# The same instructions on tiles that start at other bytes: matmul operands moved to multiples of 128

## The chip, the cores and the metric

The kernel runs on one core of one Trainium2 chip. TensorE (PE) multiplies, with its weight loads shown as an engine of their own (PEld). VectorE (DVE), ScalarE (ACT) and GpSimd (POOL) do the elementwise work. SyncE (SP) issues the transfers. The metric is the time of one execution on the device in microseconds, the median of three runs. TensorE's granted clock has two levels, 1.2 and 2.4 GHz; a share of 1.00 in the profile is the upper one.

## The reference, cut to what matters

One layer of a hybrid decoder on 512 tokens of width 1024, in float32:

```python
h = rms_norm(x, g_mix)
q, fp, iv, go, bg, cg, xc, u, v, gates = split(h @ w_in)      # 1024 x 7680
o_a = hgrn2_mix(q, fp, iv, go, lower_bounds, g_hgrn_out)      # gated linear recurrence
o_b = short_conv_mix(bg, cg, xc, w_conv)
o_c = spatial_gating_mix(u, v, sg_ln_g, sg_ln_b, w_sg, b_sg)
y = einsum('bsnw,nwd->bsnd', stack([o_a, o_b, o_c]), w_branch)
x = x + sum(sigmoid(gates) * y) @ w_o
x = x + square(relu(rms_norm(x, g_ffn) @ w_ff1)) @ w_ff2       # 1024 -> 4096 -> 1024
return rms_norm(x, g_final)
```

Nearly all of the arithmetic is in the products with `w_in`, `w_branch`, `w_o`, `w_ff1` and `w_ff2`.

## The kernel before

Activations lie with channels on the 128 partitions and the 512 tokens along the free axis, so a tile of 128 channels is 2048 bytes on each partition. Every large product is computed from split operands: a float32 value is cut into a rounded high part and the rest (`split`, L76, and `split_hi`/`split_lo`, L739 to L752; the type of both parts is float32r), and `mm3` (L88) adds three matmuls, high x high (L89), high x low (L90) and low x high (L91). One such matmul has a stationary operand of 128x128 (512 bytes on each partition, loaded by a weight load) and streams a moving operand of 128x512 through it (2048 bytes on each partition). A 1024-deep product for 128 output channels is a unit of 8 x 3 = 24 matmuls into one PSUM bank.

The work is a hand-written list of units (L537 to L555, L693 to L725). Around each unit the main loop (L858) issues the next weight tile's DMA on SP, splits the tile loaded before it on ACT and DVE, and evacuates the unit before. The recurrence, the spatial gate and the convolution hang on slots of that list (`pre`, `post`).

Where the operands lie follows from the order in which the pools hand out tiles. A tile takes a multiple of 32 bytes on each partition, and one pool's region follows the other's without a gap: first the constants (`cp`: `vec`, `cons`, `lm`, ..., `bnst`, `bnmv`), then the working pool (`wp`: three `raw`, six `tmp`, three `wh`, three `wl`, then small columns `ra` and `rr` of 16 bytes, each in a place of 32), then the slots `z`, `h` and `x` (`rp`). `raw`, `wh`, `wl` and `h` are 4096 bytes, `z` and `x` 2048. A `tmp` takes 2080 bytes, since one of its users (L489) asks for 514 columns. The constants end at byte 96 of a 128-byte line, and all that follows inherits it:

```
start modulo 128, before     raw 96 | tmp 96, 0, 32, 64, 96, 0 | wh 32 | wl 32 | z 96 | h 96 | x 96
                             ones 96 | ones_r 96 | cons 96 | wsm 96
```

Modulo 512, `wh` and `wl` start at 288, and `z`, `h` and `x` at 96. Slices of 128 or 512 columns step by multiples of 512 bytes and so keep their tile's value. The large matmuls therefore come in three kinds:

- **weights from `wh`/`wl` (32), stream from `x`, `z` or `h` (96)**: the projections, branches, output projection and the first feed-forward product; 2496 matmuls (shown as acc<-x,wh, acc<-x,wl, acc<-z,wh, acc<-z,wl, acc<-h,wh, acc<-h,wl);
- **weights from an `h` slot (96), stream from `z` (96)**: the second feed-forward product; 672 matmuls of 512 columns and 192 of 256 columns (acc<-z,h);
- **weights from `x` (96), stream from `wh`/`wl` (32)**: the two token-major products, L833 and the units of `v_mm` (L403); 192 matmuls (acc<-wh,x and acc<-wl,x).

In these names the stream stands first and the weights second. Six more float32r matmuls (L145, L146) take weights from `ones_r` (96) and stream a `tmp`; in all three at L145 that tile starts at 0. L149 is a plain float32 product of 256 columns, which the trace shows as two matmuls, each going over the columns once more slowly.

Of the kernel before, what the change touches and what calls it, by code (L numbers as in the profile page):

```python
# [7 lines left out]
F32 = mybir.dt.float32  # L8
# [5 lines left out]
P = 128  # L14
S = 512
# [21 lines left out]
def trunk_kernel(ctx: ExitStack, tc, xT, w_f, w_t, w_bc, w_a, w_o, w_1, w_2, vecs, rows, w_sg, cst, lmask, out):  # L37
    nc = tc.nc
    cp = ctx.enter_context(tc.tile_pool(name="cp", bufs=1))
    wp = ctx.enter_context(tc.tile_pool(name="wp", bufs=3))  # L40
# [7 lines left out]
    def nm(s):  # L48
        uid[0] += 1
        return f"{s}_{uid[0]}"  # L50

    def ct(shape, name, dt=F32):
        return cp.tile(shape, dt, name=name, tag=name)
# [4 lines left out]
    def zslot(i, dt):  # L58
        return rp.tile([P, S], dt, tag=f"z{i}", name=nm("z"))
# [4 lines left out]
    def acc():  # L64
        return pa.tile([P, S], F32, tag="acc", name=nm("acc"))
# [4 lines left out]
    def tt(e, o, a, b, op):  # L70
        return e.tensor_tensor(out=o, in0=a, in1=b, op=op)  # L71
# [21 lines left out]
    def cs(k, n=P):  # L93
        return slice(k * n, (k + 1) * n)

    # constants
    vec = ct([P, V_N], "vec")
    cons = ct([P, C_N], "cons")
    ident = cons[:, C_ID:C_ID + P]
# [10 lines left out]
    rb2 = ct([P, S], "rb2")  # L110

    def tmp(w=S, dt=F32):
        return wp.tile([P, w], dt, tag="tmp", name=nm("tmp"), bufs=6)

    def rsqrt_cols(src, n, inv, eps, dst):
        """dst[:, :n] = (src * inv + eps) ** -0.5"""
        a = wp.tile([P, 4], F32, tag="ra", name=nm("ra"), bufs=4)
        dve.tensor_scalar(out=a[:, :n], in0=src, scalar1=inv, scalar2=eps, op0=ALU.mult, op1=ALU.add)
        tt(pool, dst[:, :n], a[:, :n], mhalf[:, :n], ALU.pow)

    def col4():
        return wp.tile([P, 4], F32, tag="rr", name=nm("rr"), bufs=6)

    def col_sums(ps, src, n=4):
        for t in range(n):
# [2 lines left out]
    def diag(cols, n=4):  # L128
        dg = tmp()
        tt(dve, dg[:, :n * P].rearrange("p (b s) -> p b s", b=n), ident.unsqueeze(1).to_broadcast([P, n, P]),  # L130
           cols[:, :n].unsqueeze(2).to_broadcast([P, n, P]), ALU.mult)
        return dg

    def ones_hi(src):
        hi = tmp(S, F32R)
        act.activation(hi, src, AF.Copy)
        return hi

    def ones_lo(src, hi):
        lo = tmp(S, F32R)  # L140
        tt(dve, lo, src, f(hi), ALU.subtract)
        return lo
# [26 lines left out]
    units = []  # L169
# [5 lines left out]
    loads, when = [], {}  # L175
# [14 lines left out]
            return a  # L190
        return unit(w_f[j], mm, ev)

    # recurrence: decays, keys, queries
    def ev_f(h, a):
        kk[h] = zslot(2 * h, F32)
        A[h] = zslot(2 * h + 1, F32)
        hs = [hslot(h * 4 + i, F32) for i in range(4)]
        names = ("QA", "t1", "QB", "y", "q", "R", "go", "att")
        d = {n: hs[i // 2][:, cs(i % 2, S)] for i, n in enumerate(names)}
        heads.append(d)  # L200
        fp = d["QA"]
        tt(dve, fp, a, rb, ALU.mult)
        act.activation(kk[h], fp, AF.Sigmoid, scale=-1.0)
        act.activation(d["t1"], fp, AF.Abs)
        pool.memset(d["att"], 0.0)
# [55 lines left out]
            dve.tensor_scalar(out=d["y"], in0=d["y"], scalar1=al[:, h:h + 1], scalar2=cl[:, h:h + 1], op0=ALU.add, op1=ALU.max)  # L261
            tt(dve, A[h], d["y"], d["t1"], ALU.add)

    # recurrence: interactions at distance scale m = 2 ** l
    def halves(ap, m):
        v = ap.rearrange("p (b two m) -> p b two m", two=2, m=m)
        if m == 1:
            v = v[:, :, :, 0]
            return v[:, :, 0], v[:, :, 1]
        return v[:, :, 0, :], v[:, :, 1, :]  # L270
# [51 lines left out]
            mk = lm[:, cs(l)].unsqueeze(1).to_broadcast([P, 4, P])  # L322
            dve.copy_predicated(v4(d["att"]), mk, v4(d["ps"]))

    # recurrence: blocks of 128 through the state
    def far_prep(pair):
        for h in pair:
            d = heads[h]
            act.activation(d["y"][:, :3 * P], d["R"][:, :3 * P], AF.Exp)
            act.activation(d["t1"][:, P:], A[h][:, P:], AF.Exp)  # L330
        for h in pair:
            d = heads[h]
            tt(dve, d["QA"][:, :3 * P], kk[h][:, :3 * P], d["y"][:, :3 * P], ALU.mult)
            tt(dve, d["QB"][:, P:], d["q"][:, P:], d["t1"][:, P:], ALU.mult)
# [39 lines left out]
    def mix_norm(pair):  # L374
        for h in pair:
            d = heads[h]
            ss, r = col4(), col4()
            for b in range(4):
                act.activation(d["QA"][:, cs(b)], d["ps"][:, cs(b)], AF.Square, accum_out=ss[:, b:b + 1])
            rsqrt_cols(ss, 4, 1.0 / P, EPS, r)  # L380
            d["r"] = r
# [17 lines left out]
            zt[0][h] = (zslot(2 * h, F32R), zslot(2 * h + 1, F32R))  # L399
            split(d["t1"], *zt[0][h])  # L400

    # spatial gate
    def v_mm(j):  # L403
        def mm(w):
            if j == 0:
                part["v"] = [acc() for _ in range(4)]
            a4 = part["v"]
            for k2 in range(2):
                k = 2 * j + k2
                for t in range(4):  # L410
                    mm3(a4[t], xh[k][:, cs(t)], xl[k][:, cs(t)], w[0][:, cs(k2, S)], w[1][:, cs(k2, S)], k == 0, k == KD - 1)
        return mm
# [10 lines left out]

    st = ct([P, 4, 6], "bnst")
    mv = ct([P, 4, 2], "bnmv")

    def v_stats():
        for t in range(4):
            dve.bn_stats(st[:, t, :], vln[t])
            dve.bn_aggr(mv[:, t, :], st[:, t, :])  # L430

    def v_norm():
        r = col4()
        rsqrt_cols(mv[:, :, 1], 4, 1.0, LN_EPS, r)
        for t in range(4):
            dve.tensor_scalar(out=vln[t], in0=vln[t], scalar1=mv[:, t, 0:1], scalar2=r[:, t:t + 1], op0=ALU.subtract, op1=ALU.mult)
# [42 lines left out]
        zt[2][g] = (zslot(16 + 2 * g, F32R), zslot(17 + 2 * g, F32R))  # L479
        split(part["sv", g], *zt[2][g])  # L480

    # short convolution
    def ev_cg(c, a):
        y = tmp()
        part["cy"] = y
        tt(dve, y, a, rb2, ALU.mult)
# [18 lines left out]
        yield  # L505
        tt(dve, lo, y, f(hi), ALU.subtract)

    # gates, branch outputs, merge
    def ev_gate(d, n, a):
        g = tmp()  # L510
        part[n] = g
        tt(dve, g, a, rb, ALU.mult)
        act.activation(g, g, AF.Sigmoid)
# [19 lines left out]
        tt(dve, mt[:, S:], part[0], f(mt[:, :S]), ALU.subtract)  # L533
        mg.append((mt[:, :S], mt[:, S:]))

    # order of the units of tensor work
    for h in range(NH):  # L537
        proj(4 + h, lambda a, h=h: ev_f(h, a))
    for h in range(NH):
# [57 lines left out]
        at(pre, 19 + g, sg_split, g)  # L597
    at(pre, 21, go_sig)

    # output projection, residual, second norm  # L600
    x2, x2h, x2l = [], [], []

    def reload_x():
# [37 lines left out]
        ones_mm(part["c2"], part["qh"], part["ql"])  # L641

    def ffn_rows():
        """-2 * (mean square + eps) ** -0.5, on every partition"""
        a, r, t = tmp(), tmp(), tmp()
        act.activation(r, part["c2"], AF.Sqrt, scale=1.0 / D, bias=eps_c)
        dve.tensor_scalar(out=a, in0=part["c2"], scalar1=1.0 / D, scalar2=EPS, op0=ALU.mult, op1=ALU.add)
        dve.reciprocal(r, r)
        tt(pool, t, a, r, ALU.mult)
        tt(pool, t, t, r, ALU.mult)  # L650
        part["r2b"] = ct([P, S], "rb2")
        dve.scalar_tensor_tensor(out=part["r2b"], in0=t, scalar=-3.0, in1=r, op0=ALU.add, op1=ALU.mult)
# [1 line left out]
    def ffn_late():  # L654
        return [ev_1(i, held[i]) for i in range(3)]

    # feed-forward
    hid = {}

    def ev_1(i, a):  # L660
# [48 lines left out]
    at(pre, f0 + 1, ffn_split)  # L709
    at(post, f0 + 1, ffn_ss)  # L710
    at(pre, f0 + 2, ffn_rows)
    at(pre, f0 + 3, ffn_late)
    for g in range(1, NG):
# [14 lines left out]
    order = [x for s in sorted(when) for x in when[s]]  # L728
# [24 lines left out]

    held = []
    with tc.manual_schedule():
        # warm the tensor engine's clock and the activation tables while the first loads run
        dve.memset(ones, 1.0)
        pool.memset(mhalf, -0.5)
        nc.scalar.dma_start(vec, vecs)
# [2 lines left out]
        warm = acc()  # L762
        for i in range(WARM):
            pe.matmul(warm[:, :P], ones, ones, start=True, stop=True)

        # x: load, scale by the gain, split, sum of squares; the recurrence's value rows, token-major
        xr = [zslot(k, F32) for k in range(KD)]
        rw = []
        for k in range(KD):
# [17 lines left out]
        for k in range(KD + 1):  # L787
# [29 lines left out]
            if k == KD:  # L817
                cps = acc()
                col_sums(cps, sq_tot)
                rsqrt_cols(cps[:, :4], 4, 1.0 / D, EPS, rstd)  # L820
                dg = diag(rstd)
                dh = ones_hi(dg)
                dl = ones_lo(dg, dh)
# [34 lines left out]
        for i in range(len(units)):  # L858
# [27 lines left out]
            w, mm, ev = units[i]  # L886
# [4 lines left out]
                fn(*a)  # L891
        prev[0](prev[1])

        # last group of the feed-forward, by token halves, and the final norm
        g = NG - 1
        n2 = S // 2

# [31 lines left out]
        def fin_rstd():  # L929
            r = col4()  # L930
            rsqrt_cols(part["fc"][:, :2], 2, 1.0 / D, EPS, r)
            part["fd"] = diag(r, 2)
# [40 lines left out]
        warm = acc()  # L973
# [60 lines left out]
```

## Time and profile before

| | |
|---|---|
| time, median of 3 runs | 860.74 us (857.92 to 861.56) |
| profiled execution, span from first to last instruction | 859.3 us |
| its mean granted TensorE clock | 0.997 |
| PE busy | 847.2 us (99%), 3990 matmuls |
| DVE, ACT, POOL busy | 473.6, 322.3, 140.4 us |
| read from HBM | 80.83 MB, 97 GB/s over the span |

The execution's time outside of its span is not listed; the median of the runs is 1.4 us above the span. Matmuls are pipelined and their ends are modelled, so a matmul's listed duration is not what it adds to the run. What it adds is the step from its start to the next one's. The two are tied: in the timeline a matmul of 512 columns that is followed at once lasts about 163 ns more than its step, so that a mean duration of 389 ns is a step of about 226.

### The profile page before, as it was taken

To read this page: it belongs to the slowest core of one execution; us is meant where nothing else is said; L and a number is where in the kernel's file an instruction comes from. 1 tells how busy PE (TensorE), PEld (TensorE's weight loads), DVE (VectorE), ACT (ScalarE), POOL (GpSimd) and SP (SyncE) were. 2 spreads that over 40 slices of the span, in tenths; PEclk is the share of its full clock that TensorE was granted. 3 is DMA by queue.
4 is the path that set the end of the run, shared out by engine and by line. 5 is a ranking of instruction groups with operands and counts; after the bars stand their busy time and mean duration, and the time that the engine had idled before them with its cause. 6 is when DMAs were issued, how large, how long until landed. Compare 5 with 4: busy or idle time off the path is not lost.

```text
span 859.3 us, 10105 instructions
## 1 busy us (share of the span) xinstructions
PE 847.2 (99%) x3990; PEld 706.8 (82%) x3990; DVE 473.6 (55%) x623; ACT 322.3 (38%) x491; POOL 140.4 (16%) x152
## 2 busy tenths in 40 slices
PE   8999899999999999999999999999999999999997
PEld 7888788888888888888888888888888888888896
DVE  7456989978564444544445458444444444444424
ACT  6567355354333232323223446232232323232222
POOL 4313455661210000000001310000000000000034
PEclk9999999999999999999999999999999999999999
DMA  8331222212122323232235234222223232322002
GB/s 302 118 99 50 84 88 75 74 50 98 50 75 86 110 86 111 86 96 100 86 110 208 92 131 149 96 98 98 98 98 98 98 98 98 98 91 90 17 1 99
DMA packets 26256, 83.59 MB, mean 97 GB/s; under 512 B 3040, under 2 KB 3424, under 8 KB 26208
## 3 DMA queue, kind: packets, MB, share of 16 engines
q1 hardware_dynamic: 26064, 82.91, 29.1%
q8 instruction: 31, 0.51, 0.2%
q14 instruction: 17, 0.14, 0.1%
q10 hardware_dynamic: 144, 0.03, 0.0%
HBM read 80.83 MB, written 2.10 MB: 97 GB/s over the span
## 4 chain that ended last, share of the span: by engine, by line
PE 91%; DVE 3%; ACT 3%; issue 2%; DMA 0%; SPq 0%; POOL 0%; DVEq 0%; ACTq 0%
PE acc L89 28%; PE acc L91 28%; PE acc L90 28%; PE acc L317 3%; PE acc L833 1%; DVE wl L71 1%; DVE h L71 1%; ACT h L248 1%; DVE h L261 0%; DMA z<-xT 0%; ACT wh L746 0%; ACT h L252 0%; PE acc L469 0%; PE acc L370 0%; DVE h L298 0%
## 5 line engine op out<-in xcount | busy, mean ns | idle before, releaser
L89 PE MATMUL acc<-x,wh 128*128 128x512 f32 x672 | 265.5, 395 | 0.0
L90 PE MATMUL acc<-x,wh 128*128 128x512 f32 x672 | 262.7, 391 | 0.0
L91 PE MATMUL acc<-x,wl 128*128 128x512 f32 x672 | 262.7, 391 | 0.0
L746 ACT ACTIVATE wh<-raw 128x1024 fp32r<-128x1024 f32 (+1 forms) x112 | 115.0, 1028 | 377.0 <-PE acc L90 247.4
L71 DVE TENSOR_TENSOR wl<-raw,wh 128x1024 fp32r<-128x1024 f32 (+1 forms) x118 | 151.4, 1284 | 24.9 <-ACT wh L746 24.8
L91 PEld LDWEIGHTS acc<-x,wl 128*128 128x128 f32 x672 | 126.2, 188 | 28.6
L89 PEld LDWEIGHTS acc<-x,wh 128*128 128x128 f32 x672 | 126.3, 188 | 26.5
L90 PEld LDWEIGHTS acc<-x,wh 128*128 128x128 f32 x672 | 126.3, 188 | 26.4
L71 DVE TENSOR_TENSOR z<-z,acc 128x512 f32<-128x512 f32 (+1 forms) x80 | 50.6, 634 | 109.8 <-PE acc L91 109.8
L89 PE MATMUL acc<-z,h 128*128 128x512 f32 (+1 forms) x288 | 105.5, 366 | 0.0
L90 PE MATMUL acc<-z,h 128*128 128x512 f32 (+1 forms) x288 | 105.2, 365 | 0.0
L91 PE MATMUL acc<-z,h 128*128 128x512 f32 (+1 forms) x288 | 105.2, 365 | 0.0
L71 POOL TENSOR_TENSOR tmp<-tmp,tmp 128x512 f32<-128x512 f32 (+1 forms) x27 | 31.5, 1166 | 218.6 <-DVE tmp L71 186.9
L662 DVE SCALAR_TENSOR_TENSOR tmp<-acc,rb 128x512 f32<-128x512 f32 x32 | 21.9, 690 | 76.0 <-PE acc L91 76.0
L71 DVE TENSOR_TENSOR tmp<-acc,rb 128x512 f32<-128x512 f32 x28 | 19.3, 691 | 80.5 <-PE acc L91 80.5
L89 PEld LDWEIGHTS acc<-z,h 128*128 128x128 f32 x288 | 54.3, 189 | 8.8
L90 PEld LDWEIGHTS acc<-z,h 128*128 128x128 f32 x288 | 54.3, 189 | 8.8
L91 PEld LDWEIGHTS acc<-z,h 128*128 128x128 f32 x288 | 54.3, 189 | 8.7
L917 POOL TENSOR_SCALAR z<-z,vec 128x256 f32<-128x256 f32 x12 | 5.8, 484 | 312.5 <-ACT tmp L911 312.5
L663 ACT ACTIVATE tmp<-tmp 128x512 f32<-128x512 f32 x32 | 20.1, 628 | 69.2 <-DVE tmp L662 69.2
L71 DVE TENSOR_TENSOR h<-raw,h 128x1024 fp32r<-128x1024 f32 x32 | 38.9, 1217 | 0.0
L89 PE MATMUL acc<-z,wh 128*128 128x512 f32 x96 | 37.8, 394 | 0.0
(184 smaller groups left out, 984.4 us busy)
## 6 DMA issues: line engine op xcount, KB each, us to landing
raw<-w SPq DMA_DIRECT2D x64, 512.0 KB, 3.3
raw<-w_f SPq DMA_DIRECT2D x52, 512.0 KB, 3.3
raw<-w_bc SPq DMA_DIRECT2D x8, 512.0 KB, 3.3
raw<-w_o SPq DMA_DIRECT2D x8, 512.0 KB, 3.3
z<-xT SPq DMA_DIRECT2D x15, 256.0 KB, 4.3
raw<-w_t SPq DMA_DIRECT2D x4, 512.0 KB, 3.3
raw<-w_a SPq DMA_DIRECT2D x8, 256.0 KB, 2.5
out<-x SPq DMA_DIRECT2D x8, 256.0 KB, 2.1
```

Source lines behind the costliest of these rows:

```text
L71: return e.tensor_tensor(out=o, in0=a, in1=b, op=op)
L89: pe.matmul(o, lh, rh, start=start, stop=False)
L90: pe.matmul(o, lh, rl, start=False, stop=False)
L91: pe.matmul(o, ll, rh, start=False, stop=stop)
L248: act.activation(d["t1"], d["t1"], AF.Exp, scale=-1.0)
L317: pe.matmul(ps[:, cs(b)], kl[:, cs(b)], qk[:, cs(b)], start=True, stop=True)
L662: dve.scalar_tensor_tensor(out=t, in0=a, scalar=0.0, in1=part["r2b"], op0=ALU.max, op1=ALU.mult)
L663: act.activation(t, t, AF.Square, scale=0.5)
L746: act.activation(hi[:, :n], raws[i][:, :n], AF.Copy)
L833: pe.matmul(a4[t], lh, rh, start=j == 0 and rnd == 0, stop=j == KD - 1 and rnd == 2)
L917: pool.tensor_scalar(out=xv, in0=xv, scalar1=vcol(V_GFIN + d), scalar2=0.0, op0=ALU.mult, op1=ALU.add)
```

## The change

The constants pool gets one more tile of 32 bytes. A `tmp` is allocated with 544 columns (2176 bytes, 17 times 128) and used through its first `w` columns. The pool of small columns `rr` has 8 buffers in place of 6, so that `ra` and `rr` together take 12 x 32 = 384 bytes. Comments are dropped.

```diff
     def tmp(w=S, dt=F32):
-        return wp.tile([P, w], dt, tag="tmp", name=nm("tmp"), bufs=6)
+        return wp.tile([P, S + 32], dt, tag="tmp", name=nm("tmp"), bufs=6)[:, :w]
...
     def col4():
-        return wp.tile([P, 4], F32, tag="rr", name=nm("rr"), bufs=6)
+        return wp.tile([P, 4], F32, tag="rr", name=nm("rr"), bufs=8)
...
     st = ct([P, 4, 6], "bnst")
     mv = ct([P, 4, 2], "bnmv")
+    ct([P, 8], "pad")
```

The engines' instructions keep their kind, number, shape and order; the exceptions are waits: ACT has one wait instruction fewer and POOL one more, where `rr` and `tmp` buffers are taken again. What is new is where the tiles start:

```
start modulo 128, after      raw 0 | tmp 0 (all six) | wh 0 | wl 0 | z 0 | h 0 | x 0
                             ones 96 | ones_r 96 | cons 96 | wsm 96
```

Modulo 512, `wh` and `wl` now start at 384, and `z`, `h` and `x` at 256. `ones`, `ones_r`, `cons` and `wsm` lie ahead of the new tile and stay where they were.

## Rows read from the trace of the kernel before

**Rows 1.** The page, part 1: busy time, share of the span, instructions.

```profile
PE 847.2 (99%) x3990; PEld 706.8 (82%) x3990; DVE 473.6 (55%) x623; ACT 322.3 (38%) x491; POOL 140.4 (16%) x152
```

**Rows 2.** The page, part 4: the chain that ended last, by engine.

```profile
PE 91%; DVE 3%; ACT 3%; issue 2%; DMA 0%; SPq 0%; POOL 0%; DVEq 0%; ACTq 0%
```

**Rows 3.** Groups by line and shape on PE: busy us, mean ns of one.

```profile
L89 PE MATMUL acc<-z,h 128*128 128x512 f32 x224 | 87.1, 389 | 0.0
L90 PE MATMUL acc<-z,h 128*128 128x512 f32 x224 | 87.1, 389 | 0.0
L91 PE MATMUL acc<-z,h 128*128 128x512 f32 x224 | 87.1, 389 | 0.0
L89 PE MATMUL acc<-z,wh 128*128 128x512 f32 x96 | 37.8, 394 | 0.0
L91 PE MATMUL acc<-z,wl 128*128 128x512 f32 x96 | 37.6, 392 | 0.0
L90 PE MATMUL acc<-z,wh 128*128 128x512 f32 x96 | 37.2, 388 | 0.0
...
L91 PE MATMUL acc<-z,h 128*128 128x256 f32 x64 | 18.1, 283 | 0.0
...
L145 PE MATMUL acc<-tmp,ones_r 128*128 128x512 f32 x3 | 1.2, 395 | 0.0
```

**Rows 4.** Timeline of PE, three unit starts: start us, duration us.

```profile
539.51 0.39 PE L89 MATMUL acc<-z,h 128*128 128x512 f32 x1
...
561.27 0.39 PE L89 MATMUL acc<-x,wh 128*128 128x512 f32 x1
...
583.25 0.39 PE L89 MATMUL acc<-z,h 128*128 128x512 f32 x1
```

**Rows 5.** Timeline of PE, first and last matmul of three `v_mm` units.

```profile
74.99 0.39 PE L89 MATMUL acc<-wh,x 128*128 128x512 f32 x1
...
91.56 0.40 PE L91 MATMUL acc<-wh,x 128*128 128x512 f32 x1
```

**Rows 6.** Line L149: duration ns min/median/max.

```profile
L149 PE MATMUL acc<-tmp,ones x8: 377/379/483, 842.3 to 852.9; 128*128 128x256 f32 x8
```

**Rows 7.** The page, part 5: weight loads, mean ns of one.

```profile
L89 PEld LDWEIGHTS acc<-x,wh 128*128 128x128 f32 x672 | 126.3, 188 | 26.5
...
L89 PEld LDWEIGHTS acc<-z,h 128*128 128x128 f32 x288 | 54.3, 189 | 8.8
```

**Rows 8.** The chain between 0 and 110 us, in order of time.

```profile
27.32 2.91 PE acc L833 x12
...
48.36 0.23 PE acc L91
48.65 0.53 ACT h L204
...
52.56 0.93 ACT wh L746
...
94.63 1.51 DVE h L71 x3
96.27 1.96 PE acc L317 x8
```

**Rows 9.** PE's waits: us in total, times, longest us.

```profile
PE acc L317 <- DVE h L71: 3.2, 2, 2.8
```

**Rows 10.** Busy time by stretch: PE, PEld, DVE, ACT, POOL, granted clock, DMA.

```profile
75.00:105.00 30.00, 26.84 (x119) 21.77 (x118) 29.84 (x36) 12.07 (x19) 18.30 (x20) 0.94 0.22 71
105.00:230.00 125.00, 125.00 (x715) 108.91 (x714) 99.54 (x161) 61.90 (x129) 55.17 (x61) 1.00 0.22 72
...
593.00:811.00 218.00, 218.00 (x959) 179.72 (x958) 100.69 (x120) 62.41 (x78) 0.00 (x0) 1.00 0.28 90
```

## The prediction

> **What bounds the kernel now.** I read the busy shares first: PE is busy 99% of the span, DVE 55%, ACT 38% [rows 1]. Since matmul durations overlap, that alone proves little, so the chain of waits comes next: 91% of it is PE [rows 2], and among PE's waits only one is over 2 us, for DVE at the recurrence's first level [rows 9]. By stretches, PE has no gap from 105 to 811 us while DVE and ACT have room, DVE 99.5 of 125 us in its densest stretch and 100.7 of 218 in the feed-forward [rows 10]. So from 105 us on the time is the sum of the steps from one matmul's start to the next one's, and a nanosecond less on each is a nanosecond less on the span. Before that, between about 49 and 96 us, the chain runs through ACT and DVE [rows 8], and a faster PE only waits longer there.
>
> What does one step cost? The timeline gives it where a unit of known length stands between two starts [rows 4]. From 539.51 to 561.27 us lie 96 matmuls acc<-z,h: 21.76 us / 96 = 226.7 ns. From 561.27 to 583.25 lie 96 matmuls acc<-x,wh and acc<-x,wl: 21.98 / 96 = 229.0 ns. Three units of `v_mm` have 71 steps between 74.99 and 91.56 us: 16.57 / 71 = 233.4 ns [rows 5]. Clock, columns, type and accumulation are the same in all three, and the weight load is as long for `wh` as for `h`, 188 and 189 ns [rows 7]. The reader is to see that the three kinds differ in where the operands start: 96 for stream and weights (226.7), stream 96 and weights 32 (229.0), stream 32 and weights 96 (233.4). The pooled durations say the same: 389 at all three lines of acc<-z,h against a mean of 391.3 over the three of acc<-z,wh and acc<-z,wl [rows 3], which stream the same `z` slots. That leaves the weights' place, or something that goes with it, as the cause of 2.3 ns.
>
> The Trainium skill would leave nothing of this: "SBUF — State Buffer", section Door 1, gives 16 bytes as the line whose crossing costs, and 0, 32 and 96 are all multiples of 16, so that by it the change is worth nothing (860.7 us). The three step lengths above speak against it in so far as starts are what tells them apart.
>
> **The change part by part.** The new constants tile, the wider `tmp` and the two more `rr` buffers issue no work of their own. The changed waits are one on ACT and one on POOL, both on work long done; POOL is busy 16% [rows 1] and idle in the feed-forward [rows 10]. I cost them at nothing; if a POOL wait did bite it would delay a convolution product by less than one step. All that is left is the three kinds of large matmul, which now all have stream and weights at 0. No matmul of before has that pair, so its price is bounded by what is nearest.
>
> Upper bound on the step: the three matmuls at L145 stream a tile that starts at 0, with weights at 96. Their mean duration is 395 ns [rows 3], 6 above acc<-z,h, so a step of 226.7 + 6 = about 233. Lower bound: L149 needs two passes for 256 columns, each as long in the array as 512 single columns; its median is 379 ns [rows 6], 10 less than acc<-z,h, so a step of about 216. Between them stands 226.7, the step of the only kind whose two starts are equal, as they will be for all. I take that one, since it is the row nearest in kind: stream and weights in the same place within a line of 128 bytes, and the type and length of the matmuls in question.
>
> The sum, against the profiled span of 859.3 us:
> - weights from `wh`/`wl`: 2496 matmuls, of which 8 units x 24 = 192 come before 75 us. The other 2304 step down from 229.0 to 226.7: 2304 x 2.3 ns = 5.3 us, all of it on the chain.
> - acc<-z,h, 672 of 512 columns and 192 of 256: already at equal starts, 0.
> - the last `v_mm` unit, at 98 to 104 us: 24 x (233.4 - 226.7) = 0.16 us.
> - the early stretch where PE leads the chain, to 48.6 us [rows 8]: some 80 steps at 2.3 ns and the L833 matmuls, 44 steps at 6.7 ns: 0.2 + 0.3 = 0.5 us at most; I count 0.4, as some of these wait for x's DMA and split.
> - the rest before 96 us (about 110 steps at 2.3 and 72 at 6.7 ns, 0.7 us): 0, hidden behind ACT and DVE. It turns into a longer wait of L317 for DVE, now 3.2 us [rows 9].
>
> Together 5.9 us, so a span of 853.4 us. The median of the runs stands 1.4 us above the profiled span; with the same distance the time is 854.8 us, 0.7% less than 860.74.
>
> **The rivals.**
> *A misaligned stream fetches one more line each time (much faster).* The step of 226.7 ns is 544 cycles of 2.4 GHz for 512 columns, 32 too many; 32 columns are 128 bytes, and 2048 bytes from byte 96 on touch 17 lines of 128 where an aligned tile touches 16. At 256 columns the duration is 283 ns [rows 3], a step of 283 - 163 = 120 ns or 288 cycles, again 32 too many, as 9 lines instead of 8 would give. Then aligned tiles would go down to what L149 shows, about 215.7: 2304 x 13.3 = 30.6 us, 672 x 11 = 7.4, the 192 short ones 192 x 11 = 2.1, the early stretch and the last `v_mm` unit 2.2: 42.3 us, a time of 818.4. Against it: at L145 the stream already starts at 0 and the step is no shorter, and a fixed price of 32 cycles for a float32r matmul fits both lengths just as well. Half of it (pieces of 64 bytes, 6.7 ns a step) would be near 840. A sentence of the skill gives the same floor: "TensorE: Matmul & The Clock Gate", section Back-to-back issue gap, has N/2.4 + 2.5 ns, 215.8 for 512 columns; this trace's float32r rows lie above it throughout.
>
> *Nothing changes.* What tells the kinds apart could be not the place in 128 bytes but the distance of the two operands over a longer period, or which tiles are written by ACT and DVE meanwhile. Modulo 512 the distance from stream to weights goes from 192 to 128 bytes for `wh`, and stays 0 for acc<-z,h. Then `wh` keeps its 229 and the time is 859 to 861.
>
> *Offset 0 is the dear one (slower).* The rows with a stream at 0 are the three of L145, at 233. If the stream's own start sets the price, all kinds go there: 2304 x 4 ns + 672 x 6.3 + 192 x 6.3 = 9.2 + 4.2 + 1.2 = 14.6 us more, 875. For it are those rows, against it that they have weights at 96 and stand between units of another kind, with only three of them. It decides as soon as the mean step of the 2976 long matmuls from 105 us on passes 228.5 ns (what 2304 at 229.0 and 672 at 226.7 make).
>
> That the change does not do what it says touches little: `ones_r`, `ones`, `cons` and `wsm` stay at 96, but they serve six matmuls of 512 columns and short ones.
>
> **How the numbers follow.** Equal starts, 226.7 ns: 0.42, with its own range 850 to 858 (all steps 225 to 228). The line of 128 bytes, or half of it: 0.22. Nothing changes: 0.22. Offset 0 dear: 0.14. About 0.5%, 4.3 us, is what a measurement of this kernel can tell from no change, so faster begins below 856.4: the second case and three quarters and more of the first, 0.22 + 0.33 = 0.55. Within it: the rest of the first and the third, 0.09 + 0.22 = 0.31. Slower 0.14. The range of 8 in 10 takes in the line rival, down to 817, and ends at 863 above: outside stay most of the slower case and the far end of the fast one. The likeliest time is 854.8.
>
> **What would show it.** In the changed kernel's groups by line the durations of acc<-x,wh, acc<-z,wh, acc<-wh,x and acc<-z,h would all be near 389 ns, alike at L89, L90 and L91; near 379 the line rival holds; 391 to 395 for `wh` beside 389 for acc<-z,h, and nothing has changed; 395 for acc<-z,h, and offset 0 is dear. The stretch of 32 x 3 matmuls in the timeline would be 21.8 us for both kinds. L317's wait for DVE should grow by up to 0.7 us and PE's gaps from 105 us on stay at none. The forecast is wrong if acc<-z,h, whose starts were equal before and are equal after, moves at all.

## The result: slower by 0.9%

The changed kernel takes 868.62 us in the median of 4 runs (867.06 to 869.39), the kernel before 860.16 (857.92 to 861.56, 4 runs, the three given above among them). The ratio is 1.0089, 95% interval 1.0062 to 1.0116. 854.8 had been forecast, with a range of 817 to 863. Two executions in the experiments below were far slower than the others of their kernels and are left out of every time and step: one took 1425.51 us at a mean granted clock of 0.556, the other 1728.98 us, with matmul steps of 445 ns in the median though its trace gives the granted clock as 1.00.

### The profile after

The changed kernel's page, busy shares, and its chain by engine; lines behind L425 have a number one higher.

```profile
PE 855.9 (99%) x3990; PEld 709.0 (82%) x3990; DVE 474.3 (55%) x623; ACT 322.7 (37%) x491; POOL 139.6 (16%) x152
...
PE 93%; DVE 3%; ACT 3%; issue 1%; POOL 0%; DVEq 0%; ACTq 0%
```

Against [rows 1, 2] PE has the same 3990 matmuls and is busy 8.7 us longer; the other engines hardly move. The cause is in the steps. Groups by line on PE in the changed kernel (busy us, mean ns of one):

```profile
L89 PE MATMUL acc<-z,h 128*128 128x512 f32 x224 | 87.3, 390 | 0.0
L91 PE MATMUL acc<-z,h 128*128 128x512 f32 x224 | 87.3, 390 | 0.0
L90 PE MATMUL acc<-z,h 128*128 128x512 f32 x224 | 87.2, 389 | 0.0
...
L91 PE MATMUL acc<-z,wl 128*128 128x512 f32 x96 | 37.9, 395 | 0.0
L90 PE MATMUL acc<-z,wh 128*128 128x512 f32 x96 | 37.9, 395 | 0.0
L89 PE MATMUL acc<-z,wh 128*128 128x512 f32 x96 | 37.9, 395 | 0.0
```

The reader is to hold them beside [rows 3]. acc<-z,h has hardly moved (389 before), while the matmuls with weights from `wh` and `wl` went from 394, 388 and 392 to 395 at every line. The timeline of the changed kernel has the steps themselves (start us, duration us):

```profile
544.14 0.40 PE L89 MATMUL acc<-z,h 128*128 128x512 f32 x1
...
545.75 0.39 PE L90 MATMUL acc<-z,h 128*128 128x512 f32 x1
...
565.93 0.41 PE L89 MATMUL acc<-x,wh 128*128 128x512 f32 x1
...
588.25 0.40 PE L89 MATMUL acc<-z,h 128*128 128x512 f32 x1
```

96 acc<-z,h take 21.79 us, 227.0 ns a step (226.7 in [rows 4]). 96 matmuls with weights from `wh` and `wl` take 22.32 us, 232.5 a step (229.0 before). Over the whole trace the mean of the undisturbed steps (those under 245 ns) is 232.4. The acc<-z,h are dearer only at their start: the first 7 steps, up to 545.75 us, take 230.0 ns each, the other 89 take 226.7. So 2304 matmuls x 3.4 ns = 7.8 us, and 672 acc<-z,h x 0.3 to 0.4 ns = 0.2 to 0.3 us: 8.0 to 8.1 us. Measured between the medians: 8.5.

The two profiled spans differ by less, 866.1 - 859.3 = 6.8 us, since the kernel before reached its first products later in its profiled execution. The changed kernel's chain in the first 110 us shows that:

```profile
25.98 2.89 PE acc L834 x12
...
95.38 2.05 PE acc L317 x8
```

The same pieces stand at 27.32 and 96.27 us in [rows 8], so 0.9 us of the changed kernel's lead is left when the recurrence begins, and 6.8 + 0.9 = 7.7 us are lost from there on. PE's waits are the same few, L317's at DVE 2.9 us in place of 3.2 [rows 9]:

```profile
PE acc L317 <- DVE h L71: 2.9, 1, 2.9
```

### The profile page after: what moved, and what is told of

Its sections match the earlier page's. It is cut to its first block, busy times and chain, and to the rows that moved or that the text cites. A ratio compares the mean times of both kernels' runs of the same rounds, so it can differ in the third digit from the quotient of the medians.

```text
span 866.1 us, 10105 instructions
## 1 busy us (share of the span) xinstructions
PE 855.9 (99%) x3990; PEld 709.0 (82%) x3990; DVE 474.3 (55%) x623; ACT 322.7 (37%) x491; POOL 139.6 (16%) x152
## 4 chain that ended last, share of the span: by engine, by line
PE 93%; DVE 3%; ACT 3%; issue 1%; POOL 0%; DVEq 0%; ACTq 0%
PE acc L89 28%; PE acc L91 28%; PE acc L90 28%; PE acc L317 3%; PE acc L834 3%; DVE h L71 1%; DVE wl L71 1%; ACT h L248 1%; DVE h L261 0%; ACT wh L747 0%; PE acc L765 0%; ACT h L252 0%; PE acc L470 0%; PE acc L370 0%; DVE h L298 0%
## 5 line engine op out<-in xcount | busy, mean ns | idle before, releaser
L89 PE MATMUL acc<-x,wh 128*128 128x512 f32 x672 | 266.9, 397 | 0.0
L91 PE MATMUL acc<-x,wl 128*128 128x512 f32 x672 | 265.3, 395 | 0.0
L90 PE MATMUL acc<-x,wh 128*128 128x512 f32 x672 | 265.3, 395 | 0.0
L91 PEld LDWEIGHTS acc<-x,wl 128*128 128x128 f32 x672 | 126.7, 189 | 29.4
L90 PEld LDWEIGHTS acc<-x,wh 128*128 128x128 f32 x672 | 126.8, 189 | 28.7
L89 PEld LDWEIGHTS acc<-x,wh 128*128 128x128 f32 x672 | 126.7, 189 | 28.6
L89 PE MATMUL acc<-z,h 128*128 128x512 f32 (+1 forms) x288 | 105.7, 367 | 0.0
L91 PE MATMUL acc<-z,h 128*128 128x512 f32 (+1 forms) x288 | 105.4, 366 | 0.0
L90 PE MATMUL acc<-z,h 128*128 128x512 f32 (+1 forms) x288 | 105.3, 366 | 0.0
L90 PEld LDWEIGHTS acc<-z,h 128*128 128x128 f32 x288 | 54.4, 189 | 8.9
L91 PEld LDWEIGHTS acc<-z,h 128*128 128x128 f32 x288 | 54.3, 189 | 8.9
L89 PEld LDWEIGHTS acc<-z,h 128*128 128x128 f32 x288 | 54.3, 189 | 8.8
L71 DVE TENSOR_TENSOR tmp<-acc,tmp 128x512 f32<-128x512 f32 x32 | 22.0, 688 | 29.8 <-PE acc L91 29.8
```

The lines of the kernel that those rows point to most:

```text
L89: pe.matmul(o, lh, rh, start=start, stop=False)
L90: pe.matmul(o, lh, rl, start=False, stop=False)
L91: pe.matmul(o, ll, rh, start=False, stop=stop)
```

## The experiments

Only starts of tiles were moved, by unused tiles or, once, by two more buffers of `rr`. Let the distance be the byte at which the weights start less the byte at which the stream starts. Modulo 512 it was 192 before for `wh` and `wl` against `x`, `z` and `h` (288 - 96), and it is 128 after (384 - 256). acc<-z,h has 0 in both. In the third kind (weights from `x`, stream from `wh` and `wl`) the sign is the other way: 320 before, 384 after.

Three theories stood: the distance sets the step; the start of an operand within 128 bytes sets it; or the region sets it, that is, `wh` and `wl` lie far from the other slots.

### Distance 0, 128 and 192 at other starts

Distance 0 at starts of 32 modulo 128, from the kernel before:

```diff
+        rp.tile([P, 48], F32, tag="padr", name=nm("padr"))   # 192 bytes ahead of z, h, x
         xr = [zslot(k, F32) for k in range(KD)]
```

> The kernel before with one unused tile of 192 bytes ahead of the z, h and x slots, so that x, z, h start at 288 modulo 512, where wh and wl start: every pair of operands at distance 0, all at 32 modulo 128. Distance theory (the place of the weights relative to the stream within 512 bytes sets the step, 0 is best): the 2496 matmuls with weights in wh/wl step at 226.7 ns instead of 229.0, mean durations 389 to 390 at all lines, about 5.5 us faster than before, 854 to 855. Own-start theory (the start within 128 bytes of each operand by itself: 0 gave 232.4, 96 with 32 gave 229.0): the pair 32 and 32 has not been seen, and nothing makes it 226.7; acc<-z,h, now at 32 and 32 too, would move away from 226.7 with it. Region theory (wh and wl lie far from x, and z and h near each other): 229 or more stays for wh.

Measured: 855.27 us in the median of three runs (855.17 to 855.41), ratio to the kernel before 0.9936 (0.9919 to 0.9953). No steps are read of this kernel.

Distance 0 at starts of 0 modulo 128, from the changed kernel, with 128 bytes at the same place:

> The changed kernel with one unused tile of 128 bytes ahead of the z, h and x slots: all operands still at 0 modulo 128, but x, z, h at 384 modulo 512 as wh and wl, distance 0 instead of 128. Distance theory: the step of the wh/wl kinds falls from 232.4 to 226.7 ns, 2496 x 5.7 = 14 us off the changed kernel, 854 to 855, the same as the other kernel with distance 0. Own-start theory (0 modulo 128 is dear): no move, 868 to 869. Region theory: no move.

Measured: 856.37 us, ratio to the kernel before 0.9944 (0.9926 to 0.9963). The timeline of this kernel (start us, duration us):

```profile
555.82 0.39 PE L89 MATMUL acc<-x,wh 128*128 128x512 f32 x1
...
577.58 0.39 PE L89 MATMUL acc<-z,h 128*128 128x512 f32 x1
...
599.34 0.39 PE L89 MATMUL acc<-x,wh 128*128 128x512 f32 x1
```

Both groups of 96 take 21.76 us: 226.7 ns for `wh` as for `h`. All operands of the large products lie at 0 modulo 128 as in the changed kernel, and 12 us are gone. Neither the start within 128 bytes nor the region can explain that.

Distance 128 at starts of 32, from the kernel before, with 64 bytes:

> The kernel before with an unused tile of 64 bytes ahead of the z, h and x slots: x, z, h at 160 modulo 512, wh and wl at 288, distance 128 as in the changed kernel, but everything at 32 modulo 128. Distance theory: the wh/wl kinds step at 232.4 ns as in the changed kernel, 867 to 869. Own-start theory: it has the same starts modulo 128 as the kernel with distance 0 and both at 32, so the same time as that one, whichever it is. Region theory: 229, 860.

Measured: 869.3 us, ratio 1.0097 (1.0081 to 1.0113), the changed kernel's time with no operand of the large products at 0 modulo 128. Groups by line:

```profile
L90 PE MATMUL acc<-z,wh 128*128 128x512 f32 x96 | 37.9, 395 | 0.0
L91 PE MATMUL acc<-z,wl 128*128 128x512 f32 x96 | 37.9, 395 | 0.0
L89 PE MATMUL acc<-z,wh 128*128 128x512 f32 x96 | 37.9, 394 | 0.0
```

Distance 192 with `wh` and `wl` left at 0 modulo 128, from the changed kernel, with 448 bytes:

> The changed kernel with an unused tile of 448 bytes ahead of the z, h and x slots: wh and wl stay at 384 modulo 512 (0 modulo 128), x, z, h go to 192 (64 modulo 128), distance 192 as in the kernel before. Distance theory: 229.0 ns for the wh/wl kinds and a time near that of the kernel before, 860 to 861. Own-start theory: stream at 64 is new, no reason for 229.0; if the weights' start at 0 is what is dear, 232.4 stays and 868. Region theory: 232.4 stays.

Measured: 861.44 us, ratio 1.0006 (0.9995 to 1.0018), no difference from the kernel before. Its groups have the very durations of [rows 3], each at another of the three lines, so they do not belong to a line; they are three steps that repeat in turn:

```profile
L91 PE MATMUL acc<-z,wl 128*128 128x512 f32 x96 | 37.9, 394 | 0.0
L90 PE MATMUL acc<-z,wh 128*128 128x512 f32 x96 | 37.6, 392 | 0.0
L89 PE MATMUL acc<-z,wh 128*128 128x512 f32 x96 | 37.3, 388 | 0.0
```

All four times come out the way the distance theory said, 0.3 to 1.4 us above the upper end that it gave.

### Other distances, and the period

> The kernel before with an unused tile of 128 bytes ahead of z, h, x: these at 224 modulo 512, wh and wl at 288, distance 64. Distance theory in its simple form (0 is the one good place, the rest costs 2 to 7 ns): the wh/wl kinds step between 229 and 234 ns, 860 to 873. Rival, small distances are as good as 0 (the two need only be near): 226.7 and 855.

Measured: 871.58 us, ratio 1.0133 (1.0102 to 1.0164); step 233.3 ns. Group of this kernel:

```profile
L89 PE MATMUL acc<-z,wh 128*128 128x512 f32 x96 | 38.0, 396 | 0.0
```

> The kernel before with an unused tile of 448 bytes ahead of z, h, x: these at 32 modulo 512, wh and wl at 288, distance 256. If the pattern repeats every 512 bytes: a step other than 226.7, 229 to 234. If it repeats every 256 bytes: as distance 0, 226.7 and 855, and 384 would be as 128, which the early matmuls with the roles swapped allow (232.8 beside 232.4).

Measured: 854.88 us, ratio 0.9937 (0.9914 to 0.9959): the same as distance 0. The pattern repeats every 256 bytes. Groups of this kernel:

```profile
L89 PE MATMUL acc<-z,wh 128*128 128x512 f32 x96 | 37.3, 389 | 0.0
L90 PE MATMUL acc<-z,wh 128*128 128x512 f32 x96 | 37.3, 389 | 0.0
L91 PE MATMUL acc<-z,wl 128*128 128x512 f32 x96 | 37.3, 389 | 0.0
```

> The kernel before with an unused tile of 224 bytes ahead of z, h, x: these at 320 modulo 512, wh and wl at 288, distance 480, that is 32 below 0. Simple form: 229 to 234 ns, 860 to 873. If a small distance is as good as 0: 226.7 and 855. If it is better for the weights to lie a little ahead or behind, this and the distance 64 differ in sign, and one of them steps below 226.7, under 850.

Measured: 870.16 us, ratio 1.0117 (1.0087 to 1.0146); step 233.3 ns. Neither a small distance nor one of the other sign is any better. Group of this kernel:

```profile
L89 PE MATMUL acc<-z,wh 128*128 128x512 f32 x96 | 37.9, 395 | 0.0
```

> The kernel before with an unused tile of 160 bytes ahead of z, h, x: these at 256 modulo 512, wh and wl at 288, distance 32. Distance theory with a period of 256: on the other side of 0 from the measured 224, and nothing excludes a step below 226.7, but the two neighbours 64 and 224 both stand at 233.3, so 229 to 234 ns and 860 to 872.

Measured in a single run: 872.66 us, step 233.3 ns. Group of this kernel:

```profile
L89 PE MATMUL acc<-z,wh 128*128 128x512 f32 x96 | 38.0, 396 | 0.0
```

With the kind whose roles are swapped, whose distance modulo 256 is 64 before and 128 after, the map is:

```
distance modulo 256   mean undisturbed step, ns   from
0                     226.7                       acc<-z,h; both kernels with distance 0 or 256
32                    233.3                       distance 32
64                    233.3                       distance 64; the swapped kind before (320)
128                   232.4 to 233.2              changed kernel; distance 128; swapped kind after (384); moved h slots
192                   229.0, at times 233.3       kernel before (229.0); changed kernel at distance 192 (both); distance 64, swapped kind (both)
224                   233.3                       distance 480
```

### The region: moving the good kind away

```diff
+        for i in range(24): zslot(i, F32)
+        for i in range(16): xslot(i, F32)
+        rp.tile([P, 32], F32, tag="padr", name=nm("padr"))    # 128 bytes
+        for i in range(16): hslot(i, F32)
         xr = [zslot(k, F32) for k in range(KD)]
```

> The kernel before with all z and x slots laid out first, then an unused tile of 128 bytes, then the h slots: z and x stay at 96 modulo 512, h goes to 224, wh and wl stay at 288. So acc<-z,h goes from distance 0 to 128, the projections stay at 192, and the 192 matmuls acc<-h,wh go to 64. Distance theory: acc<-z,h steps at 232.4 ns instead of 226.7, 672 x 5.7 = 3.8 us and some on the short ones, acc<-x,wh stays at 229.0; 864 to 866. Region theory (wh and wl lie in a dear place, h in a good one): acc<-z,h stays at 226.7 and the time at 860 to 861.

Measured: 865.27 us in one run, with no steps to read. So it was run again:

> The kernel with the h slots at distance 128 from z once more, since the profile taken of it ran at another clock. Distance theory: acc<-z,h steps at 232.4 ns instead of 226.7, acc<-x,wh stays at 229.0, acc<-h,wh (distance 64) goes to 233.3; 864 to 866. Region theory: acc<-z,h stays at 226.7, 860 to 861.

Measured: 865.4 us, ratio 1.0055 (1.004 to 1.007). Groups by line of this kernel:

```profile
L90 PE MATMUL acc<-z,h 128*128 128x512 f32 x224 | 88.5, 395 | 0.0
L89 PE MATMUL acc<-z,h 128*128 128x512 f32 x224 | 88.5, 395 | 0.0
L91 PE MATMUL acc<-z,h 128*128 128x512 f32 x224 | 88.4, 395 | 0.0
L89 PE MATMUL acc<-z,wh 128*128 128x512 f32 x96 | 37.8, 394 | 0.0
L91 PE MATMUL acc<-z,wl 128*128 128x512 f32 x96 | 37.6, 392 | 0.0
L90 PE MATMUL acc<-z,wh 128*128 128x512 f32 x96 | 37.2, 388 | 0.0
```

acc<-z,h, the kind that had stood at 389 or 390 wherever its steps were read, goes to 395 (mean step 233.2), and acc<-z,wh keeps its 394, 388 and 392. `h` has no good region; it had a good distance.

The timeline of the same kernel holds one more thing (start us, duration us):

```profile
561.47 0.40 PE L89 MATMUL acc<-x,wh 128*128 128x512 f32 x1
...
583.86 0.39 PE L89 MATMUL acc<-z,h 128*128 128x512 f32 x1
...
606.25 0.39 PE L89 MATMUL acc<-x,wh 128*128 128x512 f32 x1
...
628.23 0.39 PE L89 MATMUL acc<-z,h 128*128 128x512 f32 x1
```

The two groups that start with acc<-x,wh are 96 matmuls each, both at distance 192. The first takes 22.39 us, 233.2 ns a step, the second 21.98 us, 229.0. So distance 192 has two steps that last for a whole stretch, and the distance alone does not say which: the changed kernel at distance 192 runs at 233.3 from 31 to 75 us and at 229.0 from 105 us on, and the swapped kind in the kernel with distance 64 (there at 192) at 233.2 from 75 to 91 us and, after a wait of PE, at about 229 from 101 to 103 us. The 229.0 of `wh` in the kernel before is one of the two. What chooses between them is not shown.

### One part of the change alone

```diff
-        return wp.tile([P, 4], F32, tag="rr", name=nm("rr"), bufs=6)
+        return wp.tile([P, 4], F32, tag="rr", name=nm("rr"), bufs=8)
```

> The kernel before with one part of the change alone: 8 buffers of rr in place of 6. The 64 bytes lie between wl and z, so the distance from x, z, h to wh, wl goes from 192 to 128, while nothing but z, h, x moves (to 32 modulo 128). Distance theory: this part alone is the whole loss, 868 to 869, wh/wl kinds at 232.4 ns. Rival, the loss comes from the starts at 0 modulo 128 or from the wider tmp: 860 to 861.

Measured: 869.49 us, ratio 1.0103 (1.0086 to 1.012). Groups of this kernel:

```profile
L90 PE MATMUL acc<-z,wh 128*128 128x512 f32 x96 | 37.9, 395 | 0.0
L91 PE MATMUL acc<-z,wl 128*128 128x512 f32 x96 | 37.9, 395 | 0.0
```

Two 32-byte places for columns of four numbers make the whole loss: the rest of the change adds nothing that can be told from the noise. They are the only part of the change that lies between `wl` and the `z`, `h` and `x` slots. The constants tile and the wider `tmp` lie ahead of `wh` and move both operands alike.

### Only the low parts at a distance

```diff
         wh = wp.tile([P, 2 * S], F32R, tag="wh", name=nm("wh"))
+        if k == 0:
+            wp.tile([P, 16], F32, tag="padw", name=nm("padw"), bufs=1)   # 64 bytes
         wl = wp.tile([P, 2 * S], F32R, tag="wl", name=nm("wl"))
```

together with a tile of 128 bytes ahead of `z`, `h`, `x`.

> The kernel before with an unused tile of 64 bytes between the wh and wl buffers and one of 128 bytes ahead of z, h, x: x, z, h and wh at 288 modulo 512 (distance 0), wl alone at 352 (distance 64). Of three matmuls in a unit one takes weights from wl. If only the distance between a stream and the weights that are read meanwhile counts: two of three pairs at distance 0, one at 64, where 233.3 was measured, so about a third of the extra 6.7 ns, a mean step of 229 and a time near 860; and the long step is that of L90 (its stream runs while the weights of L91 are loaded). If a matmul's own weights count, the long step is L91. If the first weights of a unit set the phase for all: 226.7 and 855.

Measured: 866.9 us, ratio 1.0072 (1.0052 to 1.0092). Groups by line of this kernel:

```profile
L91 PE MATMUL acc<-z,wl 128*128 128x512 f32 x96 | 38.1, 397 | 0.0
L90 PE MATMUL acc<-z,wh 128*128 128x512 f32 x96 | 37.6, 392 | 0.0
L89 PE MATMUL acc<-z,wh 128*128 128x512 f32 x96 | 37.3, 389 | 0.0
```

At L89, L90 and L91 the steps of these groups are 228.3, 229.2 and 235.8 ns, a mean of 231.1, not the 229 expected, and the time is 7 us over the 860 expected. The long one is the matmul whose own weights lie at distance 64, not the one before it, during whose stream these weights are loaded (the timeline under the account of the prediction shows the order); but its two neighbours, at distance 0, are longer than 226.7 as well. One misplaced operand in three costs two thirds of what all three cost (4.4 of 6.7 ns). What passes from one matmul to the next is not settled by this run.

## Why the prediction was wrong

**What bounds the kernel** was right. From the recurrence on the time is the sum of PE's steps, and 3.4 ns on 2304 of them came out as 7.8 of the 8.5 us. The kinds were told apart by starts, not by tiles or lines: also right, as the moved `h` slots show. One small term was off: 1.4 us were added to the span for the time of a run, and in the changed kernel's profiled run it is 1.8 (867.92 against 866.1).

**The step that failed is the price of the large matmuls**, where I took 226.7 ns "since it is the row nearest in kind: stream and weights in the same place within a line of 128 bytes". The place within 128 bytes was an assumption of mine, taken from the change and from three kinds that could not tell it from other readings. What counts is the distance, with a period of 256 bytes: 0 gave 226.7 ns at every start, and at every other distance that was tried the step was longer. With it the same three rows are told apart: acc<-z,h at 0 (226.7), `wh` at 192 (229.0), the swapped kind at 64 (233.3). The change put `wh` at 128, half a period off, where equal starts modulo 128 look alike. The step that had been put at 226.7 measured 232.4, inside the prediction's own bounds of 216 and 233; the term of 2304 matmuls, 5.3 us of gain, became 7.8 us of loss.

**The rivals.** "Nothing changes" named the right quantity, the distance over a longer period, even its values (192 to 128), and then priced the new value at nothing; no row of before had a large kind at distance 128, and I should have bounded it by the rows between 226.7 and 233.4. "Offset 0 is the dear one" had the right sign and 875 us, but its mechanism falls: with every operand at 0 the time is 856.37, with none at 0 it is 869.3. Its rows, the three at L145, had a stream at 0 and also a distance of 96 or 224 modulo 256 from the weights in `ones_r`, so that they could not tell the two apart. "A line of 128 bytes" falls as well: with stream and weights aligned to 128 the step stays at 226.7 and goes no lower in any run; at distance 128 it is 232.4.

**acc<-z,h** was to stay where it was, and moved by 0.3 to 0.4 ns. By its own sign ("if acc<-z,h ... moves at all") the forecast was wrong. The extra time lies in the first steps behind a group of another kind, 7 at 230.0 ns in the timeline above; after them the step is 226.7 again. With the neighbouring kind at distance 0 too, it is 226.7 from the first step. So what a group does to the steps is carried some steps into the next one.

**What was cost at nothing** was nothing that shows: with the `rr` buffers alone the ratio to the kernel before is 1.0103, with the waits, the wider `tmp` and the unused tile added 1.0089. The `rr` buffers issue no work, as the prediction says, but where they lie is the whole effect. The stretch from 49 to 96 us kept to ACT and DVE.

**A version that beats both kernels.** The three kernels with distance 0 or 256 take 854.9 to 856.4 us, 0.6% less than the kernel before and 1.4 to 1.6% less than the changed one, by an unused tile alone. The 226.7 ns of [rows 4] was thus the right price of a good distance, and the 5.9 us of the forecast about what such a distance gives (the three medians lie 4.4 to 5.6 us below those of the kernel before that ran beside them). That the forecast's time nearly came out in another kernel does not save its rule: equal places modulo 128 are not what gave it.

Why the distance matters is not shown. The weight load of the next matmul runs beside the stream of the present one, as the timeline of the kernel with `wl` misplaced shows (start us, duration us):

```profile
512.33 0.39 PE L90 MATMUL acc<-x,wh 128*128 128x512 f32 x1
512.34 0.19 PEld L91 LDWEIGHTS acc<-x,wl 128*128 128x128 f32 x1
512.56 0.40 PE L91 MATMUL acc<-x,wl 128*128 128x512 f32 x1
512.57 0.19 PEld L89 LDWEIGHTS acc<-x,wh 128*128 128x128 f32 x1
512.80 0.39 PE L89 MATMUL acc<-x,wh 128*128 128x512 f32 x1
```

In the changed kernel at distance 0 and in the kernel with distance 64 (acc<-z,wh and acc<-z,wl) a load starts 2 to 4 ns after a matmul, and its mean listed duration is 188 ns in both, as in [rows 7]. The extra time stands behind the load: its end is followed by the next matmul after 36 ns at distance 0 and after 43 ns at distance 64.

The Trainium skill, "TensorE: Matmul & The Clock Gate", section Part 2: What happens when you issue a matmul, says that stream and weight load have independent read ports and that loading the next weights takes nothing from the running matmul. Here the step runs from 226.7 to 233.3 ns when nothing but the place of the two to each other is changed, so the running matmul is not left untouched by where the weights lie; the measurement decides. That the two reads get in each other's way, over something that repeats every 256 bytes of a partition, is a guess. The run with `wl` alone at a distance speaks against its simplest form, since the long step there is not that of L90, whose stream runs while the weights of L91 are loaded, and so do the two steps of distance 192.

## What to carry to other kernels

When groups of the same instruction differ by a few nanoseconds, list the addresses of all their operands and ask which difference between them fits, before taking a power of two for the rule; a kind that looks "aligned" may be right by its distance from the other operand. For float32r matmuls of 512 columns with a fresh weight load each, put weights and stream at the same place modulo 256 bytes, the one distance here whose mean step was always the shortest, and look again after any edit of a small tile that lies between their pools. No other kernel was tried. A change of layout is an edit of the hot loop, even where no instruction changes.

## What the runs showed of the hardware that was not expected

- The step of a float32r matmul of 128x512 runs from 226.7 to 233.3 ns by the distance of weights and stream modulo 256 bytes. The absolute start makes no difference that these runs can show: acc<-z,h, with both operands at the same place, stood at each of the eight multiples of 32 within 256 bytes in one kernel or another, and its mean step was 226.7 to 227.1 ns at all of them.
- The step also has a memory. At distance 192 it stays at 229.0 or at 233.2 for a whole stretch, in one and the same execution; at distance 0 it comes back to 226.7 within some ten steps after a change of kind.
- The other five distances tried cost 2.3 to 6.7 ns; there is no gradual approach to 0, since 32 and 224 are as dear as 64. Distances 96 and 160 were not tried.
- For 256 columns distance 128 costs nothing. The mean durations of the three lines are 286, 282 and 281 ns, against 283 at L91 at distance 0 in [rows 3], and the undisturbed steps 118.3 to 119.2 ns against 119.8 to 119.9:

```profile
L89 PE MATMUL acc<-z,h 128*128 128x256 f32 x64 | 18.3, 286 | 0.0
L91 PE MATMUL acc<-z,h 128*128 128x256 f32 x64 | 18.0, 282 | 0.0
L90 PE MATMUL acc<-z,h 128*128 128x256 f32 x64 | 18.0, 281 | 0.0
```

These are rows of the kernel with the moved `h` slots. A weight load goes with each of them too, so the price does not come with every weight load. No other distance was tried at 256 columns.
